# A scheduler that models two DMA queues, and a new layout of the on-chip memory, in a decoder block of seven-product matrix multiplications

## The chip, the cores and the metric

The kernel runs on one core of one Trainium2 chip. The metric is the device time of one execution in microseconds, lower is better. A core has TensorE (matrix products), VectorE (called DVE), ScalarE (ACT), GpSimd (POOL) and SyncE (SP); each runs its own list of instructions in order and they wait for one another by semaphores. Here SP issues the loads of weights, and POOL issues transfers that add one on-chip tile into another.

## The reference

One decoder layer for 256 positions of width 2048, in float32: a half-step SwiGLU FFN, a mixing sub-layer of two parallel groups, and a second half-step FFN.

```python
def swiglu_ffn(x, w_gate, w_up, w_down):
    return (jax.nn.silu(x @ w_gate) * (x @ w_up)) @ w_down      # 2048 -> 5632 -> 2048

x = x + 0.5 * swiglu_ffn(rms_norm(x, ffn1_norm), ffn1_w_gate, ffn1_w_up, ffn1_w_down)
z = rms_norm(x, mix_norm) @ w_in                               # 2048 -> 5 * 1024
lru_x, lru_gate, sc_b, sc_c, sc_x = split(z)
h = rg_lru(causal_conv4(lru_x) + lru_conv_b, ...)              # gates, then a scan over positions
y_lru = h * gelu(lru_gate)
y_sc = sc_b * causal_conv3(sc_c * sc_x)
y = concat([rms_norm(y_lru, lru_out_norm), rms_norm(y_sc, sc_out_norm)])
x = x + y @ w_out                                              # 2048 -> 2048
x = x + 0.5 * swiglu_ffn(rms_norm(x, ffn2_norm), ffn2_w_gate, ffn2_w_up, ffn2_w_down)
return rms_norm(x, final_norm)
```

## The kernel before

**Precision.** A weight tile is loaded as float32 (`raw`). [...] The activations are the stationary operand and the weights the moving one; in the mixer's column halves it is the other way round.

**Seven products.** `sevens` multiplies a 2 x 2 block matrix of activations by a 2 x 2 block matrix of weights (w11, w12, w21, w22) with seven products p0 to p6 in place of eight. Sums of weights are made in place, by DVE, or by a transfer of POOL (`by_transfer`, line 643), which adds one tile to another (w12 += w22 for p6, w11 += w21 for p3). Sums of activations (`xs`, `hs`) are made once for each stage. The rows of the weights that the seven products leave over come as plain units x00, x01, x10, x11 (the first digit is which leftover block, the second which column of 512). The results collect in PSUM banks a, c, d and e; `snap` has ACT copy a bank in the middle (s5, u2, u3 in the names `s_g`, `s_u`, `u_g` of the trace), and DVE adds the copies.

**Stages of an FFN.** A hand-written opening (or, in the second FFN, `lead`) does the first 512 columns of gate and up. Then come, for s = 0, 1, 3, a `fine_stage` (layout `fine`; s = 0 does one pair of columns, the others two; each gate and each up is one `sevens`) and a `down_stage` numbered 0, 2, 4 (layout `three`), which multiplies the hidden tiles made since by rows of the down matrix. The mixer lies between the FFNs and uses the layout `two`.

**Orders.** `FINE_ORDERS[tag, s]` and `DOWN_ORDERS[tag, s]` hold a written list for each `sevens`. Its first entry is a code: j joins the banks c and e, - and others don't. The rest is TensorE's order: p and x units, T (turn the newest gated results by TensorE's transposes into hidden tiles), U (the same for the pair before), V (small vectors), n0 to n3 (turn a column for the next norm).

**The planner.** `Plan` takes steps with an engine, a length, needs and rooms, and `run` simulates them: TensorE in the written order, SP's loads by urgency, and ACT, DVE and POOL by what can begin first, the most urgent among those. The order that comes out is pinned: each engine's instructions are emitted in it. A load has a length of 0.45 on SP and a tail; a load or transfer may not end sooner than the one before plus its own share (line 237), so that both kinds go one after another.

**Places.** The stage region of each partition is 100.375 KB. `layouts` lists what lies there from the left (pairs: hi and lo of the moving weights) and from the right (raw tiles); `spans` gives their places and `hand_over` says when a place of the next stage is free. In `three`, `spare` (4 KB: the sum hs of p4, high and low) and `extra` (8 KB: the hidden tile that is needed last, m in `down_stage`) stand at the inner end of the right side, at 48.375 to 60.375 KB; the other sums lie in `keep` and the other hidden tiles in `bigs`, nine tiles of 8 KB left of the region that also hold the split weights of the x units in `fine` and the transposed inputs. Such a `bigs` tile is given out as tiles are released, and the planner does not know which.

Of the kernel before, what the change touches and what calls it, by code (L numbers as in the profile page):

```python
# [40 lines left out]
    ),  # L41
# [5 lines left out]
    ),  # L47
    (2, 0): (
        ["-", "p0", "p4", "T", "x11", "p5", "x01", "p6", "p2", "p1", "x00", "p3", "x10"],
        ["-", "p0", "p4", "x01", "p5", "x11", "p6", "p2", "x10", "p1", "p3", "x00", "T"],  # L50
# [6 lines left out]
    ),  # L57
# [9 lines left out]
        ["j", "p0", "p4", "p5", "x01", "p6", "p1", "p3", "x00", "p2"],  # L67
    ),
    (1, 2): (
        ["-", "p0", "T", "p4", "x01", "x11", "p5", "p1", "p6", "x00", "p3", "x10", "p2"],  # L70
        ["-", "p0", "p4", "p1", "x11", "p5", "x01", "p6", "p2", "p3", "x00", "x10"],
    ),
    (1, 4): (
        ["-", "p0", "T", "p4", "x01", "x11", "p5", "p1", "p6", "x00", "p2", "x10", "p3"],
        ["-", "p0", "p4", "x11", "p5", "n1", "p1", "p2", "p6", "n0", "p3", "x01", "x10", "x00"],
# [5 lines left out]
        ["j", "p0", "p4", "T", "x01", "x11", "p5", "p1", "p6", "x00", "p2", "x10", "p3"],  # L81
        ["-", "p0", "p4", "p1", "x11", "p5", "x01", "p6", "p2", "p3", "x10", "x00"],
    ),
    (2, 4): (
        ["-", "p0", "T", "p4", "x01", "x11", "p5", "p1", "p6", "x00", "p3", "x10", "p2"],
        ["-", "p0", "p4", "x01", "p5", "x11", "p6", "x00", "x10", "p2", "p3", "p1"],
# [29 lines left out]

class Plan:
# [80 lines left out]
    def run(self, margin=None):  # L198
# [2464 lines left out]
```

## Time and profile before

| | |
|---|---|
| median of 3 runs | 1726.4 us (1725.92 to 1726.5) |
| profiled execution | 1725.12 us |
| its span, first to last instruction | 1723.3 us |
| TensorE busy, share of the span | 1692.4 us, 98% |
| DVE, ACT, POOL busy | 1554.5, 1138.5, 103.0 us |
| TensorE's mean granted clock | 0.995 |
| moved by DMA | 435.51 MB |

In rows of the timeline stand the start, the length, the engine, the line, what is written and read, and in brackets the idle time before with what ended it. `out<-moving,stationary` is the form of a matmul. The line is 102 nearly everywhere, since a helper records every operation, so tiles name the work: `raw_g_w`, `hi_g_p`, `lo_g_p` are a weight of gate as loaded and split, `split_g_x` those of x units in `fine`, `hs` a sum of hidden tiles, `h` a hidden tile, `ph` a bank with a turned one; u and d in place of g mean up and down.

### The profile page before, as it was taken

Reading aid. Unit: us, or ns where it says so; the run is one execution under the profiler, and the core shown is the slowest. Engines: PE = TensorE matmul, PEld = TensorE weight load, DVE = VectorE, ACT = ScalarE, POOL = GpSimd, SP = SyncE. Lnnn points to the kernel's source line nnn. Section 1 sums busy time; section 2 is a strip of 40 time slices with the busy share of each in tenths; the row PEclk is TensorE's granted clock in tenths of the full one; section 3 lists DMA queues with packets and bytes.
Section 4 is the critical chain, followed back from the end, with each engine's and each line's share of the span. In section 5 each row is a group of like instructions: output and inputs, shape, how many; then the busy total and the mean of one; then the engine's idle time right before and its main releaser. Section 6 shows DMA issues by size and latency. Waiting matters only on the chain.

```text
span 1723.3 us, 20069 instructions
## 1 busy us (share of the span) xinstructions
PE 1692.4 (98%) x7673; PEld 1393.0 (81%) x7673; DVE 1554.5 (90%) x1269; ACT 1138.5 (66%) x1305; POOL 103.0 (6%) x130
## 2 busy tenths in 40 slices
PE   9999999999999999999999999999999999999997
PEld 7788888888788888888888888788887778878876
DVE  7999899998799999799997887898999798989997
ACT  6675666765576768588776666655666565666665
POOL 0200010000000000000000000000100000000000
PEclk9999999999999999999999999999999999999999
DMA  9797899978989989487857776997999778999984
GB/s 335 198 272 225 274 299 277 283 243 253 271 266 272 283 246 297 142 247 235 272 183 232 231 233 172 279 269 244 287 279 277 231 244 246 302 262 269 278 253 147
DMA packets 191057, 435.51 MB, mean 253 GB/s; under 512 B 8692, under 2 KB 11632, under 8 KB 187248
## 3 DMA queue, kind: packets, MB, share of 16 engines
q1 hardware_dynamic: 174912, 340.81, 56.2%
q0 software_dynamic: 15872, 92.35, 27.4%
q8 instruction: 60, 0.98, 0.2%
q10 hardware_dynamic: 176, 1.06, 0.2%
q14 instruction: 37, 0.30, 0.0%
HBM read 339.82 MB, written 2.10 MB: 198 GB/s over the span
## 4 chain that ended last, share of the span: by engine, by line
PE 69%; DVE 13%; DMA 7%; issue 6%; ACT 5%; DVEq 0%; SPq 0%; ACTq 0%
PE ps_d_a L102 8%; PE ps_u_a L102 7%; PE ps_d_c L102 5%; PE ps_g_a L102 5%; PE ps_d_d L102 4%; PE ps_g_c L102 4%; PE ps_d L102 4%; PE ps_u_d L102 3%; PE ps_u_c L102 3%; PE ps_d_e L102 3%; PE ps_in_b L102 3%; PE ps_o L102 3%; DMA raw_u_x<-in_ffn_w_up_dram 2%; ACT hi_u_p L102 2%; DVE lo_u_p L102 2%
## 5 line engine op out<-in xcount | busy, mean ns | idle before, releaser
L102 ACT CAST hi_g_p<-raw_g_w 128x1536 fp32r<-128x1536 f32 x140 | 202.1, 1476 | 119.6 <-DVE raw_g_w L102 35.8
L102 DVE TENSOR_TENSOR lo_g_p<-raw_g_w,hi_g_p 128x3072 fp32r<-128x3072 f32 (+1 forms) x90 | 236.2, 2643 | 36.2 <-ACT hi_g_p L102 17.9
L102 ACT CAST hi_u_p<-raw_u_w 128x1536 fp32r<-128x1536 f32 x140 | 202.6, 1475 | 82.8 <-DVE raw_u_w L102 64.3
L102 DVE TENSOR_TENSOR lo_u_p<-raw_u_w,hi_u_p 128x3072 fp32r<-128x3072 f32 (+1 forms) x90 | 236.6, 2643 | 6.5 <-ACT hi_u_p L102 6.4
L102 ACT CAST hi_d_p<-raw_d_w 128x1024 fp32r<-128x1024 f32 x140 | 141.1, 1047 | 104.0 <-DVE raw_d_w L102 53.1
L102 DVE TENSOR_TENSOR lo_d_p<-raw_d_w,hi_d_p 128x2048 fp32r<-128x2048 f32 (+1 forms) x90 | 161.2, 1812 | 7.0 <-ACT hi_d_p L102 6.4
L102 DVE TENSOR_TENSOR lo_d_x<-raw_d_x,hi_d_x 128x2048 fp32r<-128x2048 f32 x36 | 82.0, 2286 | 10.5 <-ACT hi_d_x L102 10.4
L102 ACT CAST hi_d_x<-raw_d_x 128x1024 fp32r<-128x1024 f32 x72 | 73.3, 1048 | 9.5 <-PE ps_u_a L102 2.5
L102 PE MATMUL ps_u_a<-hi_u_p,xT_n 128*128 128x512 f32 x280 | 70.2, 390 | 0.0
L102 PE MATMUL ps_g_a<-hi_g_p,xT_n 128*128 128x512 f32 x280 | 70.2, 390 | 0.0
L102 DVE TENSOR_TENSOR raw_g_w<-raw_g_w,raw_g_w 128x1536 f32<-128x1536 f32 x40 | 69.2, 1752 | 0.2
L102 DVE TENSOR_TENSOR raw_u_w<-raw_u_w,raw_u_w 128x1536 f32<-128x1536 f32 x40 | 69.1, 1751 | 0.0
L102 ACT CAST split_u_x<-raw_u_x 128x1024 fp32r<-128x1024 f32 x40 | 41.9, 1047 | 37.8 <-DMA raw_u_x<-in_ffn_w_up_dram 37.8
L641 POOL DMA_DIRECT2D raw_g_w<-raw_g_w x40 | 34.8, 870 | 481.1 <-DVE raw_g_w L102 221.5
L102 PEld LDWEIGHTS ps_g_a<-hi_g_p,xT_n 128*128 128x128 f32 x280 | 52.5, 188 | 11.0
L102 PEld LDWEIGHTS ps_u_a<-hi_u_p,xT_n 128*128 128x128 f32 x280 | 52.4, 188 | 10.8
L102 DVE TENSOR_TENSOR split_u_x<-raw_u_x,split_u_x 128x1024 fp32r<-128x1024 f32 x40 | 48.8, 1220 | 12.4 <-ACT split_u_x L102 12.4
L102 DVE TENSOR_TENSOR split_g_x<-raw_g_x,split_g_x 128x1024 fp32r<-128x1024 f32 x40 | 48.8, 1220 | 10.5 <-ACT split_g_x L102 10.5
L641 POOL DMA_DIRECT2D raw_u_w<-raw_u_w x40 | 34.5, 863 | 379.9 <-DMA raw_u_w<-in_ffn_w_up_dram 168.9
L102 ACT CAST split_g_x<-raw_g_x 128x1024 fp32r<-128x1024 f32 x40 | 41.9, 1047 | 17.4 <-DMA raw_g_x<-in_ffn_w_gate_dram 17.2
L102 DVE TENSOR_TENSOR raw_d_w<-raw_d_w,raw_d_w 128x1024 f32<-128x1024 f32 x40 | 48.0, 1219 | 0.2
L102 PE MATMUL ps_d<-hi_d,h 128*128 128x512 f32 x192 | 46.2, 393 | 0.0
(587 smaller groups left out, 4181.5 us busy)
## 6 DMA issues: line engine op xcount, KB each, us to landing
raw_g_w<-in_ffn_w_gate_dram SPq DMA_DIRECT2D x40, 1024.0 KB, 7.1
raw_u_w<-in_ffn_w_up_dram SPq DMA_DIRECT2D x40, 1024.0 KB, 6.9
raw_d_w<-in_ffn_w_down_dram SPq DMA_DIRECT2D x40, 1024.0 KB, 7.8
raw_d_x<-in_ffn_w_down_dram SPq DMA_DIRECT2D x36, 1024.0 KB, 7.0
raw_g_w<-raw_g_w POOLq DMA_DIRECT2D x40, 768.0 KB, 9.4
raw_u_w<-raw_u_w POOLq DMA_DIRECT2D x40, 768.0 KB, 9.1
raw_g_w<-in_ffn_w_gate_dram SPq DMA_DIRECT2D x40, 512.0 KB, 8.2
raw_g_x<-in_ffn_w_gate_dram SPq DMA_DIRECT2D x40, 512.0 KB, 4.6
```

Source lines behind the costliest of these rows:

```text
L102: ins = getattr(self.engine, name)(*args, **kwargs)
L641: nc.gpsimd.dma_start(raw[key]()[:, h, :], raw[other]()[:, h, :], accum_op=ALU.add)
```

## The change

1. `Plan` gets an object `Transfers` with two queues, `load` and `sum`. Each entry has a release time and an amount of work; when the heads of both are released, loads progress at 0.15 and sums at 0.85, and a head alone at 1. Adding an entry recomputes all ends. The state is carried from plan to plan.
2. `run` keeps counts of missing needs in place of scanning (a rewrite for the planner's own speed), with ties broken by a step's place in the list.
3. Layouts: in `three`, `spare` and `extra` go to the far left, in `fine` `tall0` does; pairs follow them. In `two` everything on the left begins 12 KB higher, since the mixer's `near` pool, left of it, gets five tiles of one kind in place of two, and `far` two in place of five.
4. `extra` counts as free from the end of the last unit that reads it, not from the end of the stage, and the plain column 3 takes the tiles in the order p, m, q in place of p, q, m.
5. Orders: most lists of `FINE_ORDERS` and `DOWN_ORDERS` are new. The code + gives a `sevens` in which DVE makes the sum for p3 in place of POOL's transfer.

```diff
 FINE_ORDERS = {
...
     (1, 1): (
-        ["-", "p0", "p4", "x01", "p5", "p2", "p6", "p1", "x11", "x00", "p3", "x10"],
+        ["-", "p0", "p4", "x01", "p5", "p2", "p6", "p1", "x11", "x10", "p3", "x00"],
         ["-", "p0", "p4", "x01", "p5", "p2", "x11", "p6", "p1", "x00", "T", "p3", "x10"],
-        ["-", "p0", "p4", "x01", "p5", "p1", "x11", "p6", "p2", "x10", "p3", "x00"],
-        ["j", "p0", "p4", "U", "x01", "p5", "p2", "x11", "p6", "x00", "p1", "p3", "x10", "T"],
+        ["-", "p0", "p4", "x01", "p5", "p1", "p6", "x11", "p2", "x10", "p3", "x00"],
+        ["j", "p0", "p4", "U", "p5", "x01", "p2", "x11", "p6", "x00", "T", "p1", "p3", "x10"],
     ),
     (1, 3): (
-        ["-", "p0", "p4", "x01", "p5", "p1", "p2", "x11", "p6", "x00", "p3", "x10"],
+        ["-", "p0", "p4", "x01", "p5", "p2", "p6", "p1", "x11", "x00", "p3", "x10"],
...
     (2, 1): (
...
-        ["j", "p0", "p4", "U", "x01", "p5", "p2", "x11", "p6", "x00", "T", "p1", "p3", "x10"],
+        ["-", "p0", "p4", "U", "p5", "x01", "p2", "x11", "p6", "x00", "p1", "T", "p3", "x10"],
...
 DOWN_ORDERS = {
...
     (1, 4): (
...
-        ["-", "p0", "p4", "x11", "p5", "n1", "p1", "p2", "p6", "n0", "p3", "x01", "x10", "x00"],
+        ["+", "p0", "p4", "n0", "x11", "p5", "p2", "x01", "p6", "n1", "p1", "x00", "p3", "x10"],
...
+class Transfers:
...
+    def flow(self, until, ended=None):
+        load, summing = self.queues["load"], self.queues["sum"]
+        while load or summing:
+            now = self.clock
+            heads = [q for q in (load, summing) if q and q[0][0] <= now]
...
+            rates = [1.0] if len(heads) == 1 else [0.15, 0.85]
+            span = min(q[0][1] / r for q, r in zip(heads, rates))
...
     def load(self, rows, fn, room):
-        step = self.add("SP", 0.45, fn, tail=1.95 + 0.68 * rows)
-        step.room, step.share = room, 0.67 * rows
+        step = self.add("SP", 0.45, fn, tail=1.5 + 0.67 * rows)
+        step.room, step.share = room, ("load", 1.35, 0.67 * rows, 0.6)
...
             if step.share is not None:
-                step.end = max(step.end, self.free.get("DMA", self.EARLY) + step.share)
-                self.free["DMA"] = step.end
+                kind, release, work, tail = step.share
+                self.transfers.add(kind, begin, begin + release, work, step, tail)
...
     layouts = {
-        "three": (["pair0", "pair1", "pair2"], ["raw2", "raw1", "raw0", "raw4", "raw3", "spare", "extra"]),
+        "three": (["spare", "extra", "pair0", "pair1", "pair2"], ["raw2", "raw1", "raw0", "raw4", "raw3"]),
         "two": (["pair0", "pair1"], ["raw2", "raw1", "raw0"]),
-        "fine": (["pair0", "pair1"], ["short", "tall0", "tall1", "tall2", "tall3"]),
+        "fine": (["tall0", "pair0", "pair1"], ["short", "tall1", "tall2", "tall3"]),
     }
...
-            z = plan.add("POOL", 2.0 if more else 1.0, lambda: moved(key, other), *needs, tail=7.4 + 0.3 * more)
-            z.share = 5.3 + 1.3 * more
+            z = plan.add("POOL", 2.0 if more else 1.0, lambda: moved(key, other), *needs, tail=6.4 + 1.28 * more)
+            z.share = "sum", 1.8, 5.11 + 1.28 * more, 0.6
...
-                return turned_parts(plan, high, low, a)
+                since = plan.ready.get("extra", Plan.EARLY) if [u] == last_hidden else Plan.EARLY
+                return turned_parts(plan, high, low, a, at=since)
...
-                    plain_column(3, [p, q, m], pairs[9:], handed)
+                    plain_column(3, [p, m, q], pairs[9:], handed)
...
-                plan.ready["extra"] = end
+                plan.ready["extra"] = max(z.end for z in last_read)
...
-                    return near.tile([P, UK, w], dt, tag="n", name=name, bufs=2)
+                    return near.tile([P, UK, w], dt, tag="n", name=name, bufs=5)
```

More of the change, by code (lines that the diff above doesn't have):

```diff
@@ L114, in __init__, with later, add @@
         self.room, self.readers, self.share, self.table = None, [], None, None
+class Transfers:
+    def __init__(self, clock):
+        self.clock = clock
+        self.queues = {"load": deque(), "sum": deque()}
+    def later(self, end):
+        moved = Transfers(self.clock - end)
+        for kind, queue in self.queues.items():
+            for release, work, step, tail in queue:
+                moved.queues[kind].append([release - end, work, step, tail])
+        return moved
+    def flow(self, until, ended=None):
[3 more added lines that the diff above has]
+            heads = [q for q in (load, summing) if q and q[0][0] <= now]
+            if not heads:
+                ahead = min(q[0][0] for q in (load, summing) if q)
+                if ahead >= until:
+                    break
+                self.clock = ahead
+                continue
+            rates = [1.0] if len(heads) == 1 else [0.15, 0.85]
+            span = min(q[0][1] / r for q, r in zip(heads, rates))
+            for q in (load, summing):
+                if q and q[0][0] > now:
+                    span = min(span, q[0][0] - now)
+            span = min(span, until - now)
+            if span <= 0:
+                break
+            self.clock = now + span
+            for q, r in zip(heads, rates):
+                q[0][1] -= span * r
+                if q[0][1] < 1e-6:
+                    z = q.popleft()
+                    if ended is not None:
+                        z[2].end = self.clock + z[3] + 0.07
+        self.clock = max(self.clock, min(until, 1e9))
+    def add(self, kind, now, release, work, step, tail):
+        self.flow(now, True)
+        self.queues[kind].append([release, work, step, tail])
+        ahead = Transfers(self.clock)
+        for k, queue in self.queues.items():
+            ahead.queues[k].extend([list(z) for z in queue])
+        ahead.flow(1e12, True)
 class Plan:
@@ L237, in run @@
             if step.share is not None:
-                step.end = max(step.end, self.free.get("DMA", self.EARLY) + step.share)
-                self.free["DMA"] = step.end
-            (order.get(step.engine) or todo[step.engine]).remove(step)
+                kind, release, work, tail = step.share
+                self.transfers.add(kind, begin, begin + release, work, step, tail)
+            if step.engine in order:
+                order[step.engine].popleft()
+            else:
+                ripe[step.engine].remove(step)
+            for z in after.get(step, ()):
+                z.missing -= 1
+                if not z.missing and z.engine not in order:
+                    ripe[z.engine].append(z)
             if step.room is not None:
@@ L256, in finish @@
             ready[f"lo{pair}"] = unit.low.end
-        return {e: f - end for e, f in self.free.items()}, {r: f - end for r, f in ready.items()}
+        free = {e: f - end for e, f in self.free.items()}
+        free["DMA"] = self.transfers.later(end)
+        return free, {r: f - end for r, f in ready.items()}
 @with_exitstack
@@ L399, in open_stage @@
             recent["raw"] = deque(raws)
-        recent["pair"] = deque([i for i in recent["pair"] if i < len(left)] + [i for i in range(len(left)) if i not in recent["pair"]])
+        pairs = sum(name[:4] == "pair" for name in left)
+        recent["pair"] = deque([i for i in recent["pair"] if i < pairs] + [i for i in range(pairs) if i not in recent["pair"]])
         opened.append(layout)
@@ L414, in hybrid_block @@
         sizes = dict(short=4, tall0=12, tall1=12, tall2=12, tall3=12, spare=4)
-        at, span = 0, {}
+        at, span = 12 if layout == "two" else 0, {}
         for name in left:
+            if name[:4] != "pair":
+                span[name] = at, at + sizes.get(name, 8)
+                at = span[name][1]
+                continue
             half = 12 if layout == "fine" else 8
```

82 lines of the change are left out of this document (48 added, 34 removed), and 14 rows, old and new, of the table FINE_ORDERS.

## Prediction

> **What bounds the kernel now.** I read the page's engine shares first, then the busy time in stretches cut at the stage borders, then TensorE's waits, then the timeline around the long ones. The page:
>
> ```profile
> span 1723.3 us, 20069 instructions
> PE 1692.4 (98%) x7673; PEld 1393.0 (81%) x7673; DVE 1554.5 (90%) x1269; ACT 1138.5 (66%) x1305; POOL 103.0 (6%) x130
> q1 hardware_dynamic: 174912, 340.81, 56.2%
> q0 software_dynamic: 15872, 92.35, 27.4%
> ```
>
> TensorE is busy for all but 30.9 us, and the change leaves every matmul in place: the same units p0 to p6 and x00 to x11 stand in each order, so 7673 stays 7673. Only two things can move the time: idle time of TensorE, and the rate at which matmuls follow each other. DVE at 90% is the next engine; it leaves some 10 us of slack in each 100.
>
> ```profile
> 0.00:60.00 60.00, 57.12 (x257) 45.50 (x257) 46.79 (x72) 37.40 (x61) 1.61 (x7) 1.00 0.80 284
> ...
> 450.00:618.00 168.00, 163.64 (x719) 134.31 (x718) 153.42 (x96) 108.80 (x101) 13.83 (x16) 0.98 0.94 276
> ...
> 1370.00:1457.00 87.00, 82.80 (x350) 66.80 (x349) 77.51 (x64) 54.66 (x62) 3.44 (x4) 0.96 0.72 215
> 1457.00:1627.00 170.00, 166.83 (x736) 136.06 (x736) 157.13 (x96) 110.19 (x101) 13.81 (x16) 1.00 0.97 288
> ...
> sum 1724.00, PE 1692.41 PEld 1392.98 DVE 1554.51 ACT 1138.51 POOL 102.99; mean PE 112.83 PEld 92.87 DVE 103.63 ACT 75.90 POOL 6.87
> ```
>
> ```profile
> 1713.90:1723.30 9.40, 0.00 (x1) 0.00 (x0) 3.61 (x10) 2.94 (x6) 0.00 (x0) 0.73 0.65 224
> ```
>
> Columns: stretch, its length, then busy time of PE, PEld, DVE, ACT, POOL. Idle in the stretches is 1724.00 - 1692.41 = 31.6 us. The opening holds 2.9 of it and is written out by hand; the output tail holds 9.4 plus 0.7 beyond the span. What is left, 31.6 - 2.9 - 9.4 - 0.7 = 18.6 us, lies in the planned stages, and three stretches hold most of it: 4.4 at 450, 4.2 at 1370, 3.2 at 1457. The waits of TensorE name who ended them:
>
> ```profile
> PE ps_g_c L102 <- ACT s_g L102: 6.4, 4, 4.1
> PE ps_d_a L102 <- ACT hi_d_p L102: 2.3, 2, 2.1
> PE ps_d_e L102 <- ACT hi_d_p L102: 2.1, 1, 2.1
> PE ps_u_c L102 <- ACT s_u L102: 1.7, 4, 0.7
> PE ps_g_c L102 <- ACT hi_g_p L102: 1.1, 2, 0.7
> ```
>
> ACT ends nearly all of them, though it is idle a third of the time: it runs a fixed order, and a piece of work stands behind one that isn't ready.
>
> **Part A, stationary tiles moved.** `extra` (the last hidden tile) and `spare` (the sum hs of p4) are stationary operands in the down stages. The spans of the layouts (lines 412 to 426) have them at 48 to 60 KB of the stage region; the change puts them at 0 to 12. Timeline and then chain of waits, down stage (1,2); read the starts, not the lengths, as a matmul's end overlaps the next:
>
> ```profile
> 378.42 2.03 PE L102 MATMUL ps_d_e<-hi_d_x,h 128*128 128x512 f32 x8
> ...
> 384.02 2.00 PE L102 MATMUL ps_d_a<-hi_d_p,hs 128*128 128x512 f32 x8
> ...
> 392.21 1.98 PE L102 MATMUL ps_d_d<-hi_d_x,h 128*128 128x512 f32 x8
> ...
> 397.65 1.98 PE L102 MATMUL ps_d_a<-hi_d_p,h 128*128 128x512 f32 x8
> ```
>
> ```profile
> 389.65 2.72 PE ps_d_a L102 x12
> ...
> 406.13 2.75 PE ps_d_c L102 x12
> 411.59 2.80 PE ps_d_c L102 x12
> ```
>
> The order here is p0, T, p4, x01, x11, p5, p1, p6, x00, p2: the unit at 378.42 is x11, on `extra`, and its 24 matmuls take 384.02 - 378.42 = 5.60 us; the one at 392.21 is x00, on a tile of `bigs`, and takes 397.65 - 392.21 = 5.44. So `extra` costs 0.16 us a unit, without any wait. Likewise 12 matmuls on the sum in `keep` (389.65) take 2.72 and those of p4 on `spare` (411.59) take 2.80; the 12 right after a slow unit (406.13) still take 2.75. Counting units that read `extra`: 4 in the first down stage (two plain columns, two x), 4 in each of the other two, 12 an FFN, 24 in all: 24 x 0.16 = 3.8 us. p4 runs five times an FFN: 10 x 0.08 = 0.8. After-effects: about 30 x 0.03 = 0.9. Sum 5.5 us, straight on TensorE, with no cover.
>
> Is the new place fast? In the mixer's column halves the weights are stationary, and lie in pair0 and pair1 of layout `two`, at 0 to 32 KB:
>
> ```profile
> 703.77 5.54 PE ps_in_x L102 x32
> 710.19 5.57 PE ps_in_x L102 x32
> ```
>
> Each is 16 matmuls of 512 columns and 16 of 256, and pair0 (0 to 16) and pair1 (16 to 32) differ by 0.03 at most: 0 to 32 KB is fast. I take the whole 5.5. The upper bound of the gain is that; the lower bound is 0 if it isn't the place. Two debts: `two` moves up by 12 KB, so pair1 there becomes 28 to 44 KB as stationary, where no row shows a stationary tile; were it as slow as `extra`, 8 units of 32 matmuls would cost 8 x 32 x 0.0067 = 1.7 us (0.0067 is 0.16 / 24); between that and 0 I take 0, nearer to the fast row at 32 KB than to 48. And the moving tiles of pair1 (`fine`) and pair2 (`three`) now reach 60 KB instead of 48; rival 4 prices it.
>
> [...]
>
> **Part B, the model of transfers.** The old planner lets loads (SP) and accumulating transfers (POOL) pass one after another; the new one lets the two heads share the engines 0.15 to 0.85. The page's queue rows say which is nearer: q1's packets take 0.562 x 1723.3 x 16 / 174912 = 89 ns each, q0's 0.274 x 1723.3 x 16 / 15872 = 476 ns; a packet of each in turn gives loads 89 / 565 = 0.16. The longest stall is such a case (DMA issues; timeline of POOL, of SP's queue; chain of waits; timeline of ACT):
>
> ```profile
> raw_in_b<-in_w_in_dram SPq DMA_DIRECT2D x8, 1024.0 KB, 5.0
> ```
>
> ```profile
> 450.02 0.86 POOL L641 DMA_DIRECT2D raw_g_w<-raw_g_w  x1 [27.91 <-DMA raw_g_w<-in_ffn_w_gate_dram]
> 451.11 0.86 POOL L641 DMA_DIRECT2D raw_g_w<-raw_g_w  x1 [0.23 <-issue]
> ```
>
> ```profile
> 450.16 0.92 SPq L102 DMA_DIRECT2D raw_g_w<-in_ffn_w_gate_dram  x2
> ```
>
> ```profile
> 450.16 11.09 DMA raw_g_w<-in_ffn_w_gate_dram
> ```
>
> ```profile
> 461.35 1.47 ACT L102 CAST hi_g_p<-raw_g_w 128x1536 fp32r<-128x1536 f32 x1 [4.45 <-DMA raw_g_w<-in_ffn_w_gate_dram]
> 462.73 0.59 ACT L102 ACTIVATE s_g<-ps_g_c 128x512 f32<-128x512 f32 x1
> ```
>
> A load of 1 MB alone lands in 5.0 us; of the two issued here, 1.5 MB together and beside two transfers, one lands after 11.09. ACT holds the cast of it (4.45 idle) ahead of the copy s_g, for which TensorE waits 4.1. A planner that knows the load is late puts s_g first: -4.1 and -0.2 of refill, -4.3. Next late is the cast itself, p1's, whose unit came right after p5 in the old order; the new one runs p2 and p6 in between, 36 matmuls or 36 x 0.227 = 8.2 us of cover against the 4.45.
>
> [...]
>
> **Part C, a wait that the new orders bring in.** The model still knows nothing of the nine shared `bigs` tiles. After U, all x units of a stage's last product use one of them, and the hidden tile turned by T must take that same one. Second FFN, order (2,1), where T stands before x10, and at the end the same place of the first FFN, where T stands last (timelines of TensorE, of ACT, of TensorE):
>
> ```profile
> 1359.06 1.04 PE L102 MATMUL ph<-ident,u_g 128*128 128x128 f32 x8
> ...
> 1370.40 0.61 PE L102 MATMUL ps_u_d<-split_u_x,xT_n 128*128 128x512 f32 x2
> 1373.12 3.54 PE L102 MATMUL ps_d_a<-hi_d_p,h 128*128 128x512 f32 x8 [2.11 <-ACT hi_d_p L102]
> 1376.45 1.33 PE L102 MATMUL ps_d_a<-lo_d_p,h 128*128 128x512 f32 x4
> 1379.87 0.51 PE L102 MATMUL ps_d_e<-hi_d_p,hs 128*128 128x512 f32 x1 [2.10 <-ACT hi_d_p L102]
> ```
>
> ```profile
> 1371.05 1.07 ACT L102 CAST h<-ph 128x512 fp32r<-128x512 f32 x2 [9.68 <-PE ps_u_d L102]
> 1372.01 2.00 ACT L102 CAST hi_d_p<-raw_d_w 128x1024 fp32r<-128x1024 f32 x2
> ```
>
> ```profile
> 366.43 2.09 PE L102 MATMUL ps_d_a<-hi_d_p,h 128*128 128x512 f32 x8
> ```
>
> The turn is done by 1360, yet the cast h waits 9.68 us until x10's last matmul ends, with hi_d_p behind it; TensorE pays 2.11 + 2.10 plus 0.3 of refill, 4.5. At 366.43, with T last, nothing is paid. The change moves T ahead of p1, p3 and x10 in (1,1) and keeps it ahead of x10 in (2,1): the 4.5 stay in the second FFN, and I add +4.5 in the first.
>
> **Part D, everything else.** Idle not yet spoken for: 18.6 - 4.1 - 4.2 = 10.3 us, in waits under 1.3 us. New orders deal these anew. Bounds: all gone, -10.3, or as many again, +10.3. I take -4.5, somewhat under half, since part of them (s_g, s_u behind casts) have the form of the 4.1. Hidden: five j orders instead of seven cost two more DVE adds of 0.7 us, and "+" in (1,4) swaps one accumulating transfer for one DVE add of 2.2 us, all beside TensorE on an engine with 10% slack; if that cover is gone they cost at most 3.6. The near and far places are 11 before and after: 0.
>
> **Sum.** Profiled execution 1725.1 (span 1723.3 and 1.8 around it): 1725.1 - 5.5 - 4.3 + 4.5 - 4.5 = 1715.3. The median stands 1.3 above that execution: 1716.6.
>
> **Rivals.**
> 1. The orders are as good as their model: C's wait doesn't come in the first FFN and 8 of D's 10.3 go. 1726.4 - 5.5 - 4.3 - 8 = 1708.6. For it: the shares fit. Against: nothing added knows `bigs`.
> 2. D is dealt anew without gain: 1726.4 - 5.5 - 4.3 + 4.5 = 1721.1.
> 3. The slow cadence isn't the place, and part A is 0: 1716.6 + 5.5 = 1722.1. Against: sums in `keep` and in `spare` have the same shape and differ. [...]
> 4. Moving tiles above 48 KB are as slow as stationary ones: by the orders some 360 matmuls of low parts in `fine` and 570 in pair2, 930 x 0.0067 = 6.2: 1722.8. Against: moving tiles reach 48 today without a trace of it.
> 5. Slower: the stall of 450 moves rather than goes. If loads put off by the new shares hold up ACT once at the head of each fine stage of s = 1 and 3, four times 4.3 instead of once, 1721.1 + 4 x 4.3 = 1738.3. It decides from three such stalls on (1721.1 + 12.9 = 1734.0). For it: ACT's fixed order stands. Against: in the three other stages none is that long today.
>
> **How the numbers follow.** Chances: forecast 0.45, rival 1 0.20, 2 0.14, 3 0.07, 4 0.05, 5 0.09. A difference under 0.2%, 3.5 us, can't be told from none. Faster means under 1722.9: the forecast, rival 1, most of 2, half of 3 and 4, 0.81; same 0.11; slower 0.08. The range, 1706 to 1725, reaches from beyond rival 1 to beyond 4 and leaves out 5.
>
> **What would show it.** A: units on `extra` at 5.44. B: at the head of (1,3), s_g ahead of the cast, no wait of 4 us. C: a long idle of ACT before a cast h near 366 and near 1370, hi_d_p behind it. Wrong if stalls above 2 us stand at new places, or if DVE's busy share nears TensorE's.

## The result: slower by 1.7%, and the profile after

The changed kernel takes 1754.2 us (1753.6 to 1756.2) beside 1726.2 for the kernel before: a ratio of 1.0168, 95% interval 1.0150 to 1.0185. 1716.6 was forecast. The profiled execution took 1753.69 us; its page:

```profile
span 1751.9 us, 20072 instructions
PE 1697.2 (97%) x7673; PEld 1392.7 (79%) x7673; DVE 1558.5 (89%) x1272; ACT 1137.6 (65%) x1305; POOL 102.2 (6%) x129
```

The 7673 matmuls are the same. Of the 28.6 us that the span grew, 23.8 are idle time of TensorE (1751.9 - 1697.2 = 54.7 where there were 30.9), and 4.8 are slower matmuls (1697.2 - 1692.4), although 24 matmuls on the stationary tile that moved now take 5.44 us where they took 5.60. DVE is no nearer to being the bound. In the names that follow `hi` is a weight that ACT's CAST has rounded to fp32r, and `lo = raw - hi` is made by DVE; with the activations split likewise, a block of 128 x 512 weights is three matmuls, two with `hi` and one with `lo`. The waits of TensorE:

```profile
PE ps_g_c L102 <- ACT hi_g_p L102: 9.5, 3, 7.6
PE ph L102 <- DVE z L102: 6.2, 2, 3.3
PE ps_u_a L102 <- ACT split_u_x L102: 5.2, 2, 2.6
PE ps_d_a L102 <- ACT hi_d_p L102: 2.3, 2, 2.1
```

The wait for s_g (6.4 in all, 4.1 the longest) is gone from the list. The first three are new or longer: before, hi_g_p came to 1.1 and split_u_x to 0.3, and z stood nowhere in the list. The fourth has the same 2.3 as before, but at another place: at 1373 before, at 379 now. Cutting both traces at the same numbered matmul shows where. First the kernel before, then the changed one (length, busy time of PE, PEld, DVE, ACT, POOL; then the clock):

```profile
60.40:135.00 74.60, 73.67 (x328) 59.76 (x329) 71.91 (x55) 55.38 (x55) 14.44 (x19) 1.00 0.93 250
...
366.10:450.20 84.10, 84.10 (x376) 69.05 (x375) 76.55 (x60) 51.93 (x59) 3.66 (x5) 1.00 0.83 252
928.20:1015.10 86.90, 86.90 (x397) 72.17 (x396) 75.64 (x80) 57.79 (x85) 1.72 (x2) 1.00 0.79 254
1015.10:1139.20 124.10, 123.23 (x555) 101.61 (x554) 109.82 (x93) 81.78 (x92) 6.90 (x8) 1.00 0.77 223
1370.20:1457.10 86.90, 82.70 (x350) 66.70 (x349) 77.61 (x64) 54.66 (x62) 3.44 (x4) 0.96 0.72 215
```

```profile
61.00:142.90 81.90, 76.58 (x329) 60.89 (x330) 72.74 (x58) 55.92 (x55) 14.48 (x19) 0.98 0.90 248
...
376.20:471.20 95.00, 87.83 (x374) 70.99 (x374) 83.10 (x66) 56.19 (x64) 4.34 (x6) 0.96 0.76 234
947.20:1037.90 90.70, 88.15 (x397) 72.03 (x396) 71.44 (x76) 53.20 (x80) 1.72 (x2) 1.00 0.66 213
1037.90:1172.40 134.50, 125.88 (x555) 102.93 (x554) 113.50 (x96) 85.14 (x96) 6.89 (x8) 0.97 0.77 225
1406.00:1488.40 82.40, 79.18 (x350) 64.24 (x348) 74.55 (x61) 52.23 (x60) 3.44 (x4) 1.00 0.78 234
```

The first product stage (1,0) costs 7.3 more, the down stage (1,2) 10.9, the lead and the fine stage (2,0) behind it 3.8 + 10.4; the down stage (2,2) costs 4.5 less. The other stages come to +0.7 together.

**The head of (2,0).** TensorE waits 7.63 us for a cast there (timeline of PE), and its first eight matmuls then take 3.78 us where eight take 1.98 elsewhere (at 392.62); the granted clock is 0.50 from 1094 to 1100:

```profile
1095.94 3.78 PE L102 MATMUL ps_g_c<-hi_g_p,xs 128*128 128x512 f32 x8 [7.63 <-ACT hi_g_p L102]
```

The loads of that stage are late. SP's queue, before and after, and the waits of SP's queue after:

```profile
1035.11 0.92 SPq L102 DMA_DIRECT2D raw_g_w<-in_ffn_w_gate_dram  x2
```

```profile
1073.38 5.05 SPq L102 DMA_DIRECT2D raw_g_w<-in_ffn_w_gate_dram  x6
```

```profile
SPq L102 <- PE ps_u L102: 11.5, 1, 11.5
```

Before, the first raw_g_w is issued long ahead; after, 11 us before its stage, when a matmul of lead (`ps_u`) releases it. That tile is `tall0`. The layouts put `spare` and `extra` at 0 to 12 KB of the stage region in `three`, and `tall0` at 0 to 12 KB in `fine`. But in the opening and in lead nothing uses `spare` and `extra`, and a pool from which no tile is taken gets no room: in the built program lead's pair0 (hi_u, lo_u) lies at 0 to 16 KB, not at 12 to 28. So `tall0` lies under pair0, while `spans` tells the planner that it is free.

**The head of (1,2).** Timelines of ACT and of TensorE:

```profile
377.35 1.07 ACT L102 CAST h<-ph 128x512 fp32r<-128x512 f32 x2 [9.92 <-PE ps_u_d L102]
378.30 2.01 ACT L102 CAST hi_d_p<-raw_d_w 128x1024 fp32r<-128x1024 f32 x2
```

```profile
376.69 0.61 PE L102 MATMUL ps_u_d<-split_u_x,xT_n 128*128 128x512 f32 x2
379.41 3.15 PE L102 MATMUL ps_d_a<-hi_d_p,h 128*128 128x512 f32 x8 [2.10 <-ACT hi_d_p L102]
382.71 1.60 PE L102 MATMUL ps_d_a<-lo_d_p,h 128*128 128x512 f32 x4
387.60 1.94 PE L102 MATMUL ph<-ident,z 128*128 128x128 f32 x8 [3.29 <-DVE z L102]
```

This is the wait that part C forecast, at its place and in its form: the cast of h stands 9.92 us behind x10's last matmul, hi_d_p behind it, and then z is late too, since DVE stood behind h.

### The profile page after: what moved, and what is told of

Read it like the earlier page. It is cut to its first block, busy times and chain, and to the rows that moved or that the text cites. A ratio compares the mean times of both kernels' runs of the same rounds, so it can differ in the third digit from the quotient of the medians.

```text
span 1751.9 us, 20072 instructions
## 1 busy us (share of the span) xinstructions
PE 1697.2 (97%) x7673; PEld 1392.7 (79%) x7673; DVE 1558.5 (89%) x1272; ACT 1137.6 (65%) x1305; POOL 102.2 (6%) x129
## 4 chain that ended last, share of the span: by engine, by line
PE 54%; DVE 17%; DMA 11%; issue 9%; ACT 6%; SPq 0%; DVEq 0%; ACTq 0%
PE ps_d_a L102 8%; PE ps_u_a L102 5%; PE ps_d_d L102 4%; PE ps_d L102 4%; PE ps_d_c L102 4%; DMA raw_u_x<-in_ffn_w_up_dram 4%; DVE lo_g_p L102 3%; PE ps_g_a L102 3%; DMA raw_g_x<-in_ffn_w_gate_dram 3%; PE ps_in_b L102 3%; PE ps_o L102 3%; PE ps_u_d L102 2%; ACT hi_u_p L102 2%; PE ps_g_c L102 2%; PE ps_u_c L102 2%
## 5 line engine op out<-in xcount | busy, mean ns | idle before, releaser
L102 ACT CAST hi_d_x<-raw_d_x 128x1024 fp32r<-128x1024 f32 x72 | 73.2, 1048 | 28.6 <-DMA raw_d_x<-in_ffn_w_down_dram 17.7
L102 DVE TENSOR_TENSOR raw_d_w<-raw_d_w,raw_d_w 128x1024 f32<-128x1024 f32 (+1 forms) x41 | 50.5, 1249 | 1.7 <-DMA raw_d_w<-in_ffn_w_down_dram 1.5
L102 PE MATMUL ps_g_c<-hi_g_p,xs 128*128 128x512 f32 x160 | 42.0, 405 | 9.5 <-ACT hi_g_p L102 9.5
```

What stands on the lines that cost most here:

```text
L102: ins = getattr(self.engine, name)(*args, **kwargs)
```

## The experiments

Layouts, lists and the planner's model of transfers were each done or undone alone. All ratios are to the kernel before, run beside each; the intervals are 95%.

| run | lists of orders | model of transfers | unused tiles | ratio (interval) |
|---|---|---|---|---|
| the change | new | new | no | 1.0168 (1.0150 to 1.0185) |
| e1_pads | new | new | yes | 1.0066 (1.0043 to 1.0089) |
| e17_T_last_no_pads | new, T last | new | no | 1.0095 (1.0062 to 1.0128) |
| e2_pads_T_last | new, T last | new | yes | 0.9993 (0.9975 to 1.0011) |
| e15_T_only | new, T alone last | new | yes | 1.0008 (0.9988 to 1.0027) |
| e7_T_last_old_model | new, T last | old | yes | 0.9970 (0.9950 to 0.9991) |
| e8_T_last_longer_sums | new, T last | new, resized | yes | 1.0340 (1.0308 to 1.0371) |
| e3_pads_old_orders | old | new | yes | 1.0086 (1.0053 to 1.0118) |
| e12_one_after_another | old | new sizes | yes | 1.0146 (1.0121 to 1.0171) |
| e13_shared_old_sizes | old | new sharing | yes | 1.0085 (1.0063 to 1.0108) |
| e6_pads_old_orders_old_model | old | old | yes | 0.9986 (0.9972 to 1.0000) |
| e4_layout | old | planner before | no | 1.0057 (1.0037 to 1.0078) |
| e5_layout_pads | old | planner before | yes | 0.9969 (0.9950 to 0.9988) |
| e10_before_T_last | old, T last | planner before | yes | 0.9927 (0.9901 to 0.9953) |
| e14_best | mixed, T last | planner before | yes | 0.9901 (0.9879 to 0.9923) |
| e16_best_lists_new_model | those of e14 | new | yes | 0.9997 (0.9979 to 1.0015) |

### The map: an empty pool takes no room

```diff
             open_stage("three", (1, 2, 0))
+            for i in range(2):
+                spare_tile(f"pad{tag}_{i}")
+            pools["extra"].tile([P, UK, 2 * S], F32R, tag="extra", name=f"pad{tag}_x")
```

> The changed kernel, with one edit: in the hand-written opening and in lead, where nothing uses spare and extra, two tiles of 2 KB and one of 8 KB are given out from them and left unused, so that the pairs stand at 12 to 60 KB, where the layout's list says, and not at 0 to 48. Theory map (an empty pool takes no room, so tall0 at 0 to 12 KB lies under pair0 in these two stages while the planner counts it as free; the first loads of the fine stage that follows wait for the last matmuls that read pair0): the stall of 7.6 us at 1087.9 goes, as do those at 59.9 and 62.3 and the slow catching up behind them, the stretches 0-143 and 1038-1172 lose some 14 us and the lead before them 1 to 3: 1754.2 - 16 = 1738 (1734 to 1742), and the first raw_g_w of (2,0) is issued near 40 us before its stage instead of 11. Rival model (the loads come late because the two-queue model orders or trusts them wrongly): no change, 1752 to 1756.

e4_layout is the kernel before with part 3 of the change (`layouts`, `spans`, near and far) and nothing else; e5_layout_pads adds the lines above to it.

> As e5_layout_pads (the kernel before with the new layouts, old planner, old orders), without the unused tiles, so that in the opening and in lead the pairs stand at 0 to 48 KB and tall0 lies under pair0. Theory map (its cost is the layout's own and needs neither the new model nor the new orders): the loads of the first raw_g_w of (1,0) and (2,0) come late as in the changed kernel, with a stall of several us at the head of (2,0): 14 to 20 us above e5_layout_pads, 1735 to 1741 where that one came in at 1721. Rival (the unused tiles helped e1_pads only because its orders leave no slack): within 3 us of e5_layout_pads.

> The kernel before with the new layouts alone (spare, extra and tall0 on the left, the mixer's near and far pools as changed) and the unused tiles of e1_pads; planner and orders as before. The stationary tiles' place by itself: 24 units on extra at 5.44 instead of 5.60 us, ten p4 on spare and their after-effects: 1726.2 - 5.5 = 1720.7 (1719.5 to 1722). If the place is not what made them slow: 1726. If the moving tiles that now reach 60 KB are slow in their turn: 1726.2 - 5.5 + 6.2 = 1727.

e1_pads measured 1.0066, a gain of 0.0102 or 17.6 us over the change. Its first raw_g_w of (2,0) is issued at 1043.68 (SP's queue of e1_pads), and the two stretches from lead to the end of (2,0) take 87.0 and 122.6 us in place of 90.7 and 134.5:

```profile
1043.68 17.27 SPq L102 DMA_DIRECT2D raw_g_w<-in_ffn_w_gate_dram  x6
```

```profile
947.60:1034.60 87.00, 87.00 (x397) 72.21 (x397) 72.64 (x78) 54.47 (x82) 1.72 (x2) 1.00 0.71 226
1034.60:1157.20 122.60, 122.60 (x555) 101.56 (x554) 112.73 (x96) 84.76 (x95) 6.89 (x8) 1.00 0.82 245
```

The expectation was wrong in one part: the stretch of (1,0) stays at 81.8. What is left there is above all a wait of 3.3 for split_u_x from 132.1 on (2.6 from 135.2 on in the changed kernel): x10's load is issued behind two loads of 1 MB of the next stage, and beside two sums, where the kernel before has one such load ahead of it. The new lists bring this wait: it stands in e7_T_last_old_model too (2.8), which has them with the old model, and not in e6_pads_old_orders_old_model, which has the old lists with that model. In e4_layout, with the old planner and the old lists, the long wait is there again (TensorE's waits):

```profile
PE ps_g_c L102 <- ACT hi_g_p L102: 9.4, 3, 7.5
```

e4_layout and e5_layout_pads differ by the unused tiles alone, 1.0057 and 0.9969, 15 us. So this cost is the layout's own, whatever the planner and the lists.
The 0.0031 of e5_layout_pads (5.3 us, between 2.1 and 8.6) holds part A, but not part A alone: the wait of 4.1 for s_g is gone there as well, and a wait of 2.4 for split_u_x and two of 2.4 together for lo_g_p are new. Part A is cleaner in the down stage (1,2), where e14_best has the lists and the planner of the kernel before and neither trace has a wait. The stretch took 84.10 there before; in e14_best:

```profile
365.70:448.90 83.20, 83.20 (x376) 69.03 (x374) 76.52 (x60) 51.86 (x59) 3.49 (x5) 1.00 0.83 254
```

That is 0.9 us less with the same 376 matmuls. Part A's terms for this stage, four units on `extra` and two p4, give 4 x 0.16 + 2 x 0.08 = 0.8 before after-effects.

### The shared tile: T before the last x unit

```diff
     (1, 1): (
-        ["j", "p0", "p4", "U", "p5", "x01", "p2", "x11", "p6", "x00", "T", "p1", "p3", "x10"],
+        ["j", "p0", "p4", "U", "x01", "p5", "p2", "x11", "p6", "x00", "p1", "p3", "x10", "T"],
     (2, 1): (
-        ["-", "p0", "p4", "U", "p5", "x01", "p2", "x11", "p6", "x00", "p1", "T", "p3", "x10"],
+        ["j", "p0", "p4", "U", "x01", "p5", "p2", "x11", "p6", "x00", "p1", "p3", "x10", "T"],
```

> As e1_pads, and the last product of (1,1) and of (2,1) has the list that (1,1) had before: U, x01, p5, p2, x11, p6, x00, p1, p3, x10, T, with c and e joined. Theory shared tile (after U the x units and the hidden tile that T makes use one tile of bigs, of which the planner knows nothing): the cast of h no longer waits for x10's matmuls, so the 9.6 us at 376 to 392 and some 4 at 1409 go, and with two units between x01 and x11 the small waits for split_u_x near 353, 361, 1382 and 1390 too: 13 to 19 us under e1_pads, 1719 to 1725 if that one comes in at 1738. Rival (the wait for z at 384 and 1409 is DVE's own lateness, not the tile's): only the waits of 2.1 and of 2 go, 3 to 5 us under e1_pads.

> The changed kernel with the two lists of e2_pads_T_last and without the unused tiles: the shared tile's cost alone. If the two causes are separate, the gain over the changed kernel (1.0168 of before) is that of e2_pads_T_last over e1_pads, 0.0073: 1.008 to 1.011, with the stall of 7.6 us at the head of (2,0) still there. If they hide one another, 1.013 or more, or 1.006 or less.

e15_T_only keeps the rest of the new lists, and e10_before_T_last starts from the old one of (2,1):

```diff
 e15_T_only
-        ["j", "p0", "p4", "U", "p5", "x01", "p2", "x11", "p6", "x00", "T", "p1", "p3", "x10"],
+        ["j", "p0", "p4", "U", "p5", "x01", "p2", "x11", "p6", "x00", "p1", "p3", "x10", "T"],
-        ["-", "p0", "p4", "U", "p5", "x01", "p2", "x11", "p6", "x00", "p1", "T", "p3", "x10"],
+        ["-", "p0", "p4", "U", "p5", "x01", "p2", "x11", "p6", "x00", "p1", "p3", "x10", "T"],
 e10_before_T_last
-        ["j", "p0", "p4", "U", "x01", "p5", "p2", "x11", "p6", "x00", "T", "p1", "p3", "x10"],
+        ["j", "p0", "p4", "U", "x01", "p5", "p2", "x11", "p6", "x00", "p1", "p3", "x10", "T"],
```

> As e1_pads (1.0066 of before); in the last product of (1,1) and of (2,1) T alone is moved to the end, and U, p5, x01, p2, x11 and the codes stay as the change has them. e2_pads_T_last (0.9993) changed both. Theory cast (all of that gain is the cast of h that stood before x10's last matmul: 9.6 us at 376 to 392, some 4 at 1409): 0.998 to 1.001. Theory both (the small waits for split_u_x and u_u near 353 to 362 and 1382 to 1392, some 2.5 us in each FFN, come from x01 and x11 with one unit between them and stay): 1.001 to 1.004.

> As e5_layout_pads (the kernel before with the new layouts and the unused tiles), with one list changed: in the last product of (2,1) T stands at the end, as it does in (1,1). Theory shared tile: the waits at 1370 to 1377 go, which cost 4.5 in the kernel before and 6 in the trace of e5_layout_pads: 4 to 6 us under it, 1715 to 1717 where it came in at 1721. Rival (the cast of h waits for something else, so that T's place changes nothing): 1721.

e2_pads_T_last gained 0.0073 over e1_pads, 12.6 us, just under the 13 to 19 expected, and e17_T_last_no_pads the same 0.0073 over the change: within the intervals the two causes add up. With T alone moved (e15_T_only) 0.0058 of it comes; between that and e2_pads_T_last the intervals overlap, so whether x01 and x11 matter is not settled. TensorE at the same place in e2_pads_T_last, without a wait:

```profile
370.46 1.03 PE L102 MATMUL ph<-ident,u_g 128*128 128x128 f32 x8
371.25 2.09 PE L102 MATMUL ps_d_a<-hi_d_p,h 128*128 128x512 f32 x8
373.17 1.08 PE L102 MATMUL ps_d_a<-lo_d_p,h 128*128 128x512 f32 x4
374.09 1.04 PE L102 MATMUL ph<-ident,z 128*128 128x128 f32 x8
```

e10_before_T_last changes T's place in (2,1) alone and gains 0.0042 over e5_layout_pads, 7 us, where 4 to 6 were expected and the prediction had put 4.5 on that stall in the kernel before. The two intervals just overlap, so the times alone don't settle that it is more than 4.5. The rows of the 12 us behind the stall show what 4.5 leaves out (busy times by stretch, the kernel before and e10_before_T_last; the last three columns are clock, DMA share, GB/s):

```profile
1372.00:1384.00 12.00, 8.79 (x23) 6.44 (x24) 11.96 (x14) 8.70 (x11) 0.86 (x1) 0.72 0.26 53
```

```profile
1371.90:1384.00 12.10, 12.10 (x61) 10.12 (x60) 12.10 (x13) 7.02 (x11) 0.86 (x1) 1.00 0.79 203
```

TensorE waits 2.11 + 2.10 = 4.2 us at these two places. The granted clock of the first stretch is 0.72, which by an estimate from that row (12 us, 1 - 0.72) takes up to 12 x 0.28 = 3.4 more, 7.6 together. In the second stretch, which has no stall, the clock is 1.00.

### The model of the two queues

e3_pads_old_orders is e1_pads with all lists as before; e6_pads_old_orders_old_model and e7_T_last_old_model take the planner's transfers back as well:

```diff
-        step = self.add("SP", 0.45, fn, tail=1.5 + 0.67 * rows)
-        step.room, step.share = room, ("load", 1.35, 0.67 * rows, 0.6)
+        step = self.add("SP", 0.45, fn, tail=1.95 + 0.68 * rows)
+        step.room, step.share = room, 0.67 * rows
...
             if step.share is not None:
-                kind, release, work, tail = step.share
-                self.transfers.add(kind, begin, begin + release, work, step, tail)
+                step.end = max(step.end, self.free.get("DMA", self.EARLY) + step.share)
+                self.free["DMA"] = step.end
...
-            z = plan.add("POOL", 2.0 if more else 1.0, lambda: moved(key, other), *needs, tail=6.4 + 1.28 * more)
-            z.share = "sum", 1.8, 5.11 + 1.28 * more, 0.6
+            z = plan.add("POOL", 2.0 if more else 1.0, lambda: moved(key, other), *needs, tail=7.4 + 0.3 * more)
+            z.share = 5.3 + 1.3 * more
```

> As e1_pads, with all lists of orders as they were before; the two-queue model, the layouts and the readiness of extra stay new. If the orders carry the whole rest of the loss and the model is neutral: the time before less the faster cadence, 1726.2 - 5.5 = 1720.7 (1718 to 1723). If the model gains as forecast at the head of (1,3) (4.3 us): 1716. If the model itself makes loads late: 1726 or more, with long waits for casts whose loads landed beside two transfers.

> As e3_pads_old_orders (old orders, new layouts with the unused tiles), and the transfers are planned as before: a load ends after 1.95 + 0.68 a block of rows, loads and sums one after another. What stays new against e5_layout_pads is the readiness of extra, the tie-break and the order p, m, q. Theory model (the two-queue model itself, with its shorter landing times, costs the 20 us by which e3_pads_old_orders stands above e5_layout_pads): back to 1721 (1719 to 1724). Rival small print (the readiness of extra, which lets the planner use that tile before the stage's end, or the tie-break costs them): stays at 1736 to 1742.

> As e2_pads_T_last (new orders but for the two last products, new layouts with the unused tiles), with the transfers planned as before. Theory model: the stalls of e2 at 337, 458 to 463, 513 to 519, 619 and 1345 (casts whose loads land after the planner's time) shrink, and the time falls by 8 to 12 us to about 1714. Rival (the new orders need the new model, with which they were searched): 1730 or more, with stalls of casts ahead of copies as at 458.8 in the kernel before.

With the old lists the new model costs 0.0100, 17 us (e3_pads_old_orders against e6_pads_old_orders_old_model): of the three outcomes named for e3, it is the one in which the model itself makes loads late. The readiness of extra, the tie-break and the order p, m, q, all that parts e6 from e5_layout_pads, change nothing that the intervals can tell. With the new lists the model costs 0.0023, and there the intervals overlap; the 8 to 12 us expected of e7_T_last_old_model didn't come. Two runs split it, from e3_pads_old_orders: e12 takes the rule `step.end = max(...)` of the diff above with the new sizes, e13 keeps the two queues with the old ones:

```diff
 e12_one_after_another
+        step.room, step.share = room, 0.67 * rows
+            z = plan.add("POOL", 2.0 if more else 1.0, lambda: moved(key, other), *needs, tail=6.51 + 0.28 * more)
+            z.share = 5.11 + 1.28 * more
 e13_shared_old_sizes
+        step = self.add("SP", 0.45, fn, tail=1.95 + 0.68 * rows)
+        step.room, step.share = room, ("load", 1.35, 0.68 * rows, 1.05)
+            z.share = "sum", 1.8, 5.3 + 1.3 * more, 1.3
```

> As e3_pads_old_orders, with half of the new model: the new, shorter landing times of a load or sum alone (2.02 + 0.67 a block of rows for a load; 7.58 and 8.86 for a sum), but loads and sums one after another as before. With e13_shared_old_sizes it splits the 17 us between e3_pads_old_orders (two queues, new sizes: 1.0086 of before) and e6_pads_old_orders_old_model (one after another, old sizes: 0.9986). Theory sharing (a load beside a sum gets 0.15, the planner takes the tile for late and puts other work ahead of its cast in ACT's fixed order, though it lands earlier): this one comes out near e6, 0.997 to 1.001 of before. Theory sizes (the planner trusts a load 0.45 us before it lands): near e3, 1.006 to 1.011.

> The other half: as e3_pads_old_orders, with the two queues and their shares of 0.15 and 0.85, but a load or sum alone lands when the planner before thought (2.47 + 0.68 a block of rows; 8.47 and 9.77). Theory sharing: as slow as e3_pads_old_orders or slower, 1.007 or more of before. Theory sizes: near e6, 0.997 to 1.001.

Neither theory holds for both runs: e13 came as the theory of sharing has it, e12 fits neither. The new sizes alone cost 0.0160, the sharing alone 0.0099, both together 0.0100. Each half brings a loss by itself, and the halves don't add up; what inside the model costs the time stays open. Then the sizes were set by the traces:

```diff
-            rates = [1.0] if len(heads) == 1 else [0.15, 0.85]
+            rates = [1.0] if len(heads) == 1 else [0.2, 0.8]
-        step = self.add("SP", 0.45, fn, tail=1.5 + 0.67 * rows)
+        step = self.add("SP", 0.45, fn, tail=2.0 + 0.67 * rows)
-            z.share = "sum", 1.8, 5.11 + 1.28 * more, 0.6
+            z.share = "sum", 1.8, 5.11 + 2.56 * more, 1.2
```

> As e2_pads_T_last, with the two-queue model kept and its sizes corrected by the traces: the two sums of a fine stage move 1.5 MB, which at the 197 GB/s of the rows take 7.7 us and not 6.4 (5.11 + 2.56 in place of 5.11 + 1.28), a load lands 0.5 later (tail 2.0 and 1.1 in place of 1.5 and 0.6), a sum 0.6 later, and a load beside a sum gets 0.2 in place of 0.15. If the loss of the model is its sizes: 8 to 12 us under e2_pads_T_last, about 1714. If it is the sharing itself: no change, 1722 to 1728.

1.0340: 60 us more than e2_pads_T_last, where 8 to 12 less were expected. Its rows show, in one case, how an estimate that is too late can cost time. In e8_T_last_longer_sums, SP's queue, the DMA issue in that moment, ACT, and TensorE:

```profile
108.67 0.37 SPq L102 DMA_DIRECT2D raw_u_x<-in_ffn_w_up_dram  x1
```

```profile
raw_u_x<-in_ffn_w_up_dram SPq DMA_DIRECT2D x1, 512.0 KB, 4.0
```

```profile
114.49 1.48 ACT L102 CAST hi_u_p<-raw_u_w 128x1536 fp32r<-128x1536 f32 x1 [2.66 <-PE ps_u_a L102]
115.87 0.59 ACT L102 ACTIVATE u_u<-ps_u_a 128x512 f32<-128x512 f32 x1
116.36 1.46 ACT L102 CAST hi_u_p<-raw_u_w 128x1536 fp32r<-128x1536 f32 x1
117.72 1.04 ACT L102 CAST split_u_x<-raw_u_x 128x1024 fp32r<-128x1024 f32 x1
```

```profile
118.82 0.50 PE L102 MATMUL ps_u_e<-split_u_x,xT_n 128*128 128x512 f32 x1 [3.00 <-ACT split_u_x L102]
```

The tile lands at 108.67 + 4.0 = 112.7. Its cast runs 5 us later, since three other pieces, one of which itself waits 2.66 for TensorE, stand ahead of it on ACT; TensorE waits 3.00. The planner's own times for the two kernels say why: it reckons that this load lands 8.3 us after its start here, and 5.2 us in e2_pads_T_last, where it is issued at about 106.8 and its cast runs at 111.27, ahead of those pieces. A load taken for late is put behind others, the order is fixed, and the stall that was planned becomes real. Only this case was followed. The largest group of TensorE's waits in this run is of the same kind (22.8 us in eight waits for split_u_x, in bank e); the rest of the 60 us was not traced to a cause.

### Putting it together

From e10_before_T_last to e14_best:

```diff
     (1, 1): (
-        ["-", "p0", "p4", "x01", "p5", "p2", "p6", "p1", "x11", "x00", "p3", "x10"],
+        ["-", "p0", "p4", "x01", "p5", "p2", "p6", "p1", "x11", "x10", "p3", "x00"],
...
-        ["-", "p0", "p4", "x01", "p5", "p1", "x11", "p6", "p2", "x10", "p3", "x00"],
+        ["-", "p0", "p4", "x01", "p5", "p1", "p6", "x11", "p2", "x10", "p3", "x00"],
     (2, 0): (
-        ["-", "p0", "p4", "T", "x11", "p5", "x01", "p6", "p2", "p1", "x00", "p3", "x10"],
-        ["-", "p0", "p4", "x01", "p5", "x11", "p6", "p2", "x10", "p1", "p3", "x00", "T"],
+        ["-", "p0", "p4", "T", "x11", "p5", "x01", "p6", "p1", "p2", "x00", "p3", "x10"],
+        ["-", "p0", "p4", "x01", "p5", "x11", "p6", "p2", "x10", "p1", "p3", "T", "x00"],
```

> As e10_before_T_last (0.9927 of before), with the new lists of (1,1) and of (2,0), the last product of (1,1) with T at the end as before. In the stages of e7_T_last_old_model these lists took 5.6 and 1.7 us less than the old ones in e5_layout_pads. If that is the orders': 1715.1 - 5 = 1710, 0.989 to 0.991 of before. If it was the chance landing of one load (x11's at 344 in (1,1), beside two sums): 0.992 to 0.994, no change.

> The lists of e14_best (0.9901 of before with the planner as it was) in the changed kernel's planner: two-queue model, new sizes, readiness of extra; layouts and unused tiles as in e14_best. Theory model (the new model makes any lists dearer, by the 10 thousandths between e3_pads_old_orders and e6_pads_old_orders_old_model): 0.998 to 1.002. Theory fit (lists suit the model under which they were chosen; half of these were chosen under each): 0.992 to 0.996. If the new model is as good as the old one: 0.989 to 0.992.

e14_best takes 1711.5 us, 0.9901 of the kernel before: the planner before, the new layouts with the unused tiles, T last in (1,1) and (2,1), and the new lists otherwise in (1,1) and (2,0). It is the fastest of all; its interval overlaps that of e10_before_T_last, so what the lists of (1,1) and (2,0) add is not settled. Its page:

```profile
span 1705.2 us, 20069 instructions
PE 1680.8 (99%) x7673; PEld 1388.3 (81%) x7673; DVE 1554.8 (91%) x1269; ACT 1139.1 (67%) x1305; POOL 103.2 (6%) x130
```

The same lists under the new model (e16_best_lists_new_model) take 0.9997: the model, here with the readiness of extra, the tie-break and the order p, m, q, costs 0.0096, as with the old lists.

The way from the kernel before to the changed one, in steps of ratios from the runs: the layouts with the unused tiles -0.0031 (e5; part A and the waits that shifted with it); the new lists with T kept last, old model, with the tie-break and the readiness and order of points 2 and 4 of the change +0.0001 (e7 less e5); the new model +0.0023 (e2 less e7); T moved ahead +0.0073 (e1 less e2); the empty pools +0.0102 (the change less e1). Sum 0.0168; in microseconds -5, 0, +4, +13, +18. The second and the third are within their intervals; the last two, the place of T and the empty pools, are clear of them.

## Why the prediction was wrong, step by step

**Part A was right in place and size.** In the changed kernel x11 of (1,2), on `extra`, and p4, on `spare` (timelines of TensorE):

```profile
398.06 1.98 PE L102 MATMUL ps_d_e<-hi_d_x,h 128*128 128x512 f32 x8
...
403.50 0.84 PE L102 MATMUL ps_d_a<-hi_d_p,hs 128*128 128x512 f32 x3
```

```profile
430.70 1.98 PE L102 MATMUL ps_d_e<-hi_d_p,hs 128*128 128x512 f32 x8
...
433.42 0.84 PE L102 MATMUL ps_d_d<-hi_d_p,h 128*128 128x512 f32 x3
```

5.44 us for 24 matmuls (5.60 before) and 2.72 for 12 (2.80 before). Neither debt came: the mixer's stretch takes 225.1 us after and 225.0 before, and its groups of 32 matmuls take 5.54 and 5.57 as before (at 722.75 and 729.17), so pair1 at 28 to 44 KB cost nothing as stationary, and with moving tiles up to 60 KB the units keep their 5.44, which ends rival 4. Rival 3 falls with these units: the same shape on the same engine took 5.60 at the old place and 5.44 at the new one. So the time went with the place in these runs; whether it is the address, or what lies and is written beside it, no run parts.

**The step that failed is one the prediction didn't take.** It priced the layouts by the times of matmuls at their places alone, and its last word on them was "The near and far places are 11 before and after: 0." Moving a pool, the runs show, also moves what the next stage's tiles lie under, and the list of a layout was taken for the layout. 17.6 us, more than half of the loss of 28, came in there. Who must leave the new place of `tall0` before its load can start was not asked.

**Part C was right in its place and its cause, and too small.** 4.5 were added for (1,1); the stretch of (1,2) took 10.9 more. The term counted the waits and 0.3 of refill. Missing was the clock behind them: 0.72 in the kernel before at 1372 to 1384, so that the 4.5 there were 7 to 9 (e10_before_T_last: 0.0042, and 78.1 us in that stretch in place of the 86.8 of e5_layout_pads). And in (1,2) z comes 3.29 late as well.

Behind the wait of 7.63 at the head of (2,0) eight matmuls take 3.78 us, where eight take 1.98. Behind a wait of only 2.10, in the row at 379.41, eight take 3.15, at a granted clock of 0.50 from 381 to 383. Yet the length of a wait alone doesn't decide it. At the same place of the second FFN TensorE waits 2.90, the next eight on `hi_d_p` take 2.09, and the granted clock of 1406 to 1488.4 is 1.00; why is open:

```profile
1412.42 1.22 PE L102 MATMUL ph<-ident,z 128*128 128x128 f32 x8 [2.90 <-DVE z L102]
1413.40 2.09 PE L102 MATMUL ps_d_c<-hi_d_p,hs 128*128 128x512 f32 x8
```

In the second FFN the forecast was that the 4.5 stay. They shrank: hi_d_p stands ahead of the cast of h in the changed kernel's ACT order, and the stretch takes 82.4 in place of 86.9.

**Part B: the stall went, but not by the model.** It is gone in e5_layout_pads too, which has the planner before. POOL's and SP's queue at the head of (1,3), in e4_layout, where it stands, and in e5_layout_pads, each followed by ACT:

```profile
451.56 0.86 POOL L646 DMA_DIRECT2D raw_g_w<-raw_g_w  x1 [27.45 <-DMA raw_g_w<-in_ffn_w_gate_dram]
```

```profile
451.71 0.92 SPq L102 DMA_DIRECT2D raw_g_w<-in_ffn_w_gate_dram  x2
```

```profile
463.49 1.47 ACT L102 CAST hi_g_p<-raw_g_w 128x1536 fp32r<-128x1536 f32 x1 [5.05 <-DMA raw_g_w<-in_ffn_w_gate_dram]
```

```profile
453.16 0.86 POOL L646 DMA_DIRECT2D raw_g_w<-raw_g_w  x1 [27.45 <-DMA raw_g_w<-in_ffn_w_gate_dram]
```

```profile
453.10 0.92 SPq L102 DMA_DIRECT2D raw_g_w<-in_ffn_w_gate_dram  x2
```

```profile
460.15 1.48 ACT L102 CAST hi_g_p<-raw_g_w 128x1536 fp32r<-128x1536 f32 x1 [0.31 <-DMA raw_g_w<-in_ffn_w_gate_dram]
```

Where the sum is issued 0.15 us ahead of the load, the cast waits 5.05; where the load is 0.06 ahead, 0.31. In the kernel before, too, the sum is 0.14 ahead and the cast waits 4.45. So issues 0.2 us apart (0.15 + 0.06) went with waits over 4 us apart, and in e5_layout_pads nothing was planned to that end: the stall went by luck. What was forecast, s_g ahead of the cast, didn't come in the changed kernel either. There ACT still runs two casts of hi_g_p (476.47) ahead of s_g (479.44); the load goes 4 us ahead of the sum (465.77 against 469.76), and TensorE waits for nothing from 471 to 500. e7_T_last_old_model, with the same list and the old model, has no stall there either. The share of 0.16 was an estimate from the packets of the page (89 and 476 ns), with a packet of each queue in turn; no run shows such turns, and the model with 0.15 didn't make the plan better.

**Part D** had -4.5 for new lists. With the shared tile kept out of it the new lists are worth nothing under the old model as a whole (+0.0001, from two ratios known to 0.002 each), though those of (1,1) and (2,0) may be (e14_best). Under the new model they are 0.0093 better than the old lists (e2_pads_T_last against e3_pads_old_orders), about what the old lists lose by it. The prediction gave that model no cost at all, and here it cost 4 us with the new lists, within the intervals, and 17 with the old ones. **Rival 5** named the right side, and its mechanism didn't come: no stall stands at the heads of the fine stages of s = 1 and 3. The sign given for a wrong prediction, stalls over 2 us at new places, was met at 135.2, 384.3, 626.2, 1088.3 and 1409.5.

What stays open: why the two halves of the model don't add up, and why a model whose shares are nearer to the estimate from the packets costs more. What is shown is its size with three sets of lists (with the new ones within the intervals), and in one case (e8_T_last_longer_sums) the form that it takes.

## What to carry to other kernels

When a change moves on-chip tiles, look up in the built program, for every stage, what really lies where: a pool that is empty in one stage shifts all that stands behind it, and a planner with a written map plans loads into rooms that aren't free. Price a stall of TensorE with the matmuls behind it, and read their clock: here two waits of 4.2 us in all came with a clock of 0.72 over 12 us, by the estimate above up to 3.4 us more, while behind one of 2.90 it was 1.00. A more exact model of one resource is no gain by itself in a planner whose order is fixed afterwards: a tile taken for late can cost a stall as a late one does (3.00 us in the case that was followed), and the old lists, which came with the old model, lost 17 us under the new one.

## What the runs showed of the hardware

- Behind its waits of 2.11 and 2.10 us in the kernel before, TensorE's granted clock was 0.50 from 1373.5 to 1376.5 and from 1381 to 1383, and 0.72 over the 12 us from 1372 on; behind the wait of 2.90 at 1409.5 in the changed kernel it stayed at 1.00. Its mean over the span was 0.995 in the kernel before, 0.992 in the changed kernel and 0.999 in e14_best. By an estimate the 0.007 between the last two is 0.007 x 1752 = 12 us.
- In the down stage (1,2) of the kernel before, 24 matmuls took 5.60 us with their stationary tile at 48 to 60 KB of the stage region and 5.44 with it on a tile of `bigs`. With that tile at 0 to 12 KB, in the changed kernel, they took 5.44, and the units with moving tiles up to 60 KB took 5.44 as well.
- Loads of 512 KB beside two sums took unequal times: at the same place and with the same lists in (1,1), x11's took 7.8 us in the kernel before (issued at 332.82, the sums at 336.49 and 338.36) and 15.6 in e10_before_T_last (332.12, 335.79 and 339.30); the shortest of its kind in the kernel before took 3.6.
